# The first expert pair gathered in fp32 from x kept on chip, a norm weight as a column, and another order at the end of the first block's attention

## The chip, the cores and the metric

One Trainium2 chip, one of its cores. The metric is the device time of one execution in microseconds; the kernel is timed in several runs and their median is taken. A single execution has also been profiled.

## What is computed

256 tokens of width 1024 pass a first block (three mixers side by side, then a feed-forward net), a second block (two attentions with gates), a mixture of 32 experts in 4 groups, and a last norm. Cut to what the change touches:

```python
# first block: 6 GDN heads, 6 NSA heads, 4 pooling groups, concatenated, projected, added to x
o = rms_norm(o, norm_g) * jax.nn.silu(heads(z))          # gated norm of the GDN heads, norm_g is (64,)
y = jnp.concatenate([y_a, y_b, y_c], axis=-1)
x = x + y @ w_out
x = x + square(relu(rms_norm(x, norm_ffn) @ w_ffn1)) @ w_ffn2
# second block ends with x = x + (...) @ w_o; then, on h = rms_norm(x, g_moe):
#   a router picks 2 experts in each of the chosen groups, with weights;
#   x = x + sum over picked e of weight_e * ((silu(h @ w1[e]) * (h @ w3[e])) @ w2[e])
# out = rms_norm(x, g_final)
```

## The kernel before

The activations x lie on chip in the tile `xt` (128 partitions, two token tiles of 1024 fp32). Matmuls of the dense parts take operands split in two: `split` (L285 to L299) writes a high half `wh` (a copy with rounding, on POOL at L295 or on ACT at L297, in turn when no engine is named) and a low half `wl` (the difference, DVE, L298); three products, L302 to L304, make one full product. `lin_tok` runs such a product over eight chunks of rows.

The order of the first block is written by hand: `ORDER1` (L27) is a list of names, each of which advances one generator by a step. Names used below: `z` (the gate projection; SiLU parts on ACT, last step on DVE at L550), `fin` (finish of the GDN heads: the norm's scale `rO`, made on POOL at L312 from the sums `ssO` at L1273; the multiply y by rO at L1276; then per token tile z by the norm weights on POOL, L1284, and y by z on DVE, L1285; then six transposes `py` on PE at L1291, whose evacuations L1293 and L1294 make the two halves of `yT`), `pm` (pool mix: running sums on POOL at L683 to L689, a matmul at L693), `cmp` and `no` (the compressed branch of NSA and its output; `pcs` L910/L916, `poc` L941), `y` (load of w_out) and `o` (w_out itself, over chunks 6, 7, 0 to 5; chunks 6 and 7 need the pool mix alone).

The second block ends with `out` (L1582): w_o in column blocks; after each block `Router.part` (L1678) squares x (ACT, L1682), transposes it (`phT`, L1689), evacuates it to `hT` in turn on DVE and ACT (L1695, L1693), and makes the router's logits (`plg`, L1698); and `parts` (L1572 to L1580) splits x into three bf16 parts `xp` on POOL (copy, difference, copy, difference; L1577 to L1580). `finish` adds the residual x to the output banks on PE (L1717) and picks experts on DVE (L1729 to L1739, ending in the mask `A`), then ranks tokens with `prk` (PE, L1744).

`moe` (L1781) runs 16 pairs of experts with 64 slots each. Per pair: `slots` makes one-hot matrices `oh` (bf16 on DVE, L1815; an fp32 copy on ACT, L1820), `gather` picks the tokens by matmuls of xp with the one-hot matrix (six bf16 matmuls for each of eight chunks, L1829) and DVE writes `xe` (L1830); `first` makes `ph` with W1, `third` `ph3` with W3; `ppt` transposes the one-hot matrices, ACT copies them to `pT` (L1893) and applies SiLU (L1898), DVE multiplies into `a` (L1901), `pgt` transposes a (L1909), ACT evacuates it to `gT` (L1911), and `po_e` applies W2. The gather of the next pair lies ahead of and behind `pgt`. All expert matmuls are issued through the helper at L1802.

The experts' weights come in tiles of 1 MB (`Experts`, SLOTS of 23 tiles), issued on SP's queue in one fixed order; each transfer waits until what lay in its slot is no longer needed, and what stands behind it in the queue waits with it. 13 tiles are put ahead of the pairs, the rest of the first 23 as memory comes free at the end of the second block; from then on a slot is filled again when its pair has used it.

Of the kernel before, what the change touches and what calls it, by code (L numbers as in the profile page):

```python
# [108 lines left out]
def _params(I):  # L109
# [13 lines left out]
    rest = [("gng", row(I["gdn_norm"])),  # L123
# [22 lines left out]
_P2_SHAPES = (("gng", 64), ("qcol", 1), ("kcol", 3), ("krow", 64), ("posT", 32), ("w2c", 256), ("pw", 128), ("psc", 2))  # L146
# [23 lines left out]
def fused_kernel(ctx, tc, I, out, dbg=None):  # L170
# [36 lines left out]
    xt = cs2.tile([P, 2, D], F32, name="xt")  # L207
# [229 lines left out]
def block1(K):  # L437
# [4 lines left out]
    with ExitStack() as st1:  # L442
# [119 lines left out]
        def w_out():  # L562
# [402 lines left out]
class Gdn:  # L965
# [312 lines left out]
    def finish(self, z, yT):  # L1278
# [3 lines left out]
        for t in range(2):  # L1282
            zv = z[:, t].rearrange("p (h d) -> p h d", h=H)
            G.tensor_tensor(zv, zv, bc(K.PR("gng"), (P, H, 64), 1), op=OP.mult)  # L1284
            V.tensor_tensor(y[:, t], y[:, t], zv, op=OP.mult)  # L1285
            yield
        K.dump("y_a", y)
        for a in range(3):
# [4 lines left out]
            S.activation(yT[0][:, a], pf, AF.Copy)  # L1293
            V.tensor_tensor(yT[1][:, a], pf, yT[0][:, a].bitcast(F32), op=OP.subtract)  # L1294
# [14 lines left out]
def block2(K):  # L1309
# [4 lines left out]
    with ExitStack() as st:  # L1314
# [257 lines left out]
        def parts(i, t, c0, c1):  # L1572

            a, b, c = [K.xp[:, t, j, :, 16 * c0:16 * c1] for j in range(3)]
            x = xt[:, t, c0 * P:c1 * P].rearrange("p (q c) -> p c q", c=8)
            d = K.hp.tile([P, 512], F32, name="xd", bufs=2)[:, :(c1 - c0) * P].rearrange("p (c q) -> p c q", c=8)
            G.tensor_copy(a, x)  # L1577
            G.tensor_tensor(d, x, a, op=OP.subtract)
            G.tensor_copy(b, d)
            G.tensor_tensor(c, d, b, op=OP.subtract)  # L1580

        def out():  # L1582
            K.router = Router(K)
            for i, (c0, c1) in enumerate(OUT):
# [75 lines left out]
class Router:  # L1660
# [89 lines left out]
    def weights(self):  # L1750
# [14 lines left out]
        S.activation(gx, gx, AF.Exp)  # L1765
        x = x.rearrange("p t g e -> p t (g e)")
# [12 lines left out]
def moe(K):  # L1779
# [8 lines left out]
    with ExitStack() as st:  # L1788
# [3 lines left out]
        with tc.tile_pool(name="wx", bufs=1, reuse_waits="tile") as wx, \  # L1792
# [14 lines left out]

            def slots(p_):

                o = wx.tile([P, 2, 2, CAP], F32, name="oh")  # L1810
                ob = wx.tile([P, 2, 2, CAP], BF16, name="ohb")
                sl = bc(bc(C("IOTA1")[:, :CAP], (P, 2, CAP), 1), (P, 2, 2, CAP), 1)
                if p_ == 0:
                    for t in range(2):
                        V.scalar_tensor_tensor(ob[:, t], bc(rt.pr[:, t, :2], (P, 2, CAP), 2), 256.0, sl[:, t],  # L1815
                                               op0=OP.add, op1=OP.is_equal)
                    rt.last = V.scalar_tensor_tensor(rk, rt.pr, 256.0, rt.A.rearrange("p t g e -> p t (g e)"), op0=OP.add, op1=OP.mult)
                else:
                    V.tensor_tensor(ob, sl, bc(rk[:, :, 2 * p_:2 * p_ + 2], (P, 2, 2, CAP), 3), op=OP.is_equal)
# [322 lines left out]
```

## Time and profile before

| | |
|---|---|
| median of 3 runs | 1039.4 us (1038.61 to 1040.7) |
| profiled execution | 1036.04 us, span 1034.1 us |
| granted clock, mean | 0.99 |
| busy: PE, DVE, ACT, POOL | 989.6, 461.6, 277.3, 228.9 us |
| read from HBM | 289.87 MB |

Times in the rows below are microseconds from the start of the span. A row of a timeline has the start, the time to the end of the last instruction of the row, engine, line, operation, output and inputs, the count, and in brackets how long the engine had been idle and who released it. Wait rows give the engine and line that waited, whom it waited for, the total, the number of waits and the longest. [...]

### The profile page before, as it was taken

The page shows a single profiled execution, that of the slowest core. Times are in us where ns is not written, and L with a number is a line of the kernel's source. Part 1 is how long each engine was busy: PE and PEld are TensorE (multiplying, and loading weights), DVE is VectorE, ACT ScalarE, POOL GpSimd, SP SyncE. Part 2 cuts the span into 40 slices and gives each one's busy share as a digit, 9 for nine tenths or more (in the row PEclk, how much of TensorE's full clock was granted, in tenths as well). Part 3 has the DMA queues.
Part 4 walks back from the last instruction along what each step waited for, and adds up shares of the span by engine and source line. Part 5 has one row for each costly group of instructions (what it writes and reads, how often), then busy time and mean ns, then how long its engine had stood idle before and what let it go on. Part 6 is the DMA issues. An engine that isn't in the chain of part 4 may idle for free. (4 is left out here: it accounts for less than half of the span.)

```text
span 1034.1 us, 16556 instructions
## 1 busy us (share of the span) xinstructions
PE 989.6 (96%) x6613; PEld 686.2 (66%) x6613; DVE 461.6 (45%) x948; ACT 277.3 (27%) x635; POOL 228.9 (22%) x318
## 2 busy tenths in 40 slices
PE   7999988999999999999999899999999999999995
PEld 6778766899988888887788434444444555555352
DVE  3878866665566653567688511111111111111012
ACT  3543333433333342435343011111101111111012
POOL 3682442222222225443337400000000000000000
PEclk9999997999999999999999999999999999999998
DMA  9552363755555554365677799999999999999994
GB/s 345 146 167 94 107 182 129 282 176 191 184 189 198 177 170 153 123 204 175 222 259 312 272 394 421 420 419 420 421 421 418 421 420 421 419 419 420 420 410 179
DMA packets 81999, 292.61 MB, mean 283 GB/s; under 512 B 11584, under 2 KB 26240, under 8 KB 58880
## 3 DMA queue, kind: packets, MB, share of 16 engines
q1 hardware_dynamic: 80768, 289.68, 73.9%
q10 hardware_dynamic: 1152, 1.86, 0.5%
q8 instruction: 53, 0.87, 0.3%
q14 instruction: 26, 0.21, 0.1%
HBM read 289.87 MB, written 1.64 MB: 282 GB/s over the span
## 5 line engine op out<-in xcount | busy, mean ns | idle before, releaser
L1802 PE MATMUL ph<-w,xe 128*64 128x512 f32 x1024 | 227.0, 593 | 2.3 <-DMA w<-in_w_dram 2.3
L1802 PEld LDWEIGHTS ph<-w,xe 128*64 128x64 f32 x1024 | 85.5, 137 | 132.5 <-issue 124.7
L1802 PE MATMUL po_e<-w,gT 128*64 128x512 f32 x528 | 115.1, 584 | 0.7 <-ACT gT L1911 0.7
L298 DVE TENSOR_TENSOR wl<-ffn,wh 128x512 fp32r<-128x512 f32 (+1 forms) x100 | 84.6, 849 | 62.4 <-ACT wh L297 31.3
L312 POOL TENSOR_TENSOR r<-r4a,mhalf 128x2 f32<-128x2 f32 x1 | 0.7, 698 | 442.1 <-DVE r4a L310 442.1
L1896 DVE COPY ws<-ppt 64x2 f32<-64x2 f32 x32 | 5.0, 157 | 194.8 <-ACT pT L1893 194.6
L1802 PEld LDWEIGHTS po_e<-w,gT 128*64 128x64 f32 x528 | 40.1, 136 | 63.8 <-issue 55.9
L295 POOL TENSOR_SCALAR wh<-ffn 128x512 fp32r<-128x512 f32 (+1 forms) x50 | 44.5, 890 | 138.3 <-PE acc_c L405 61.1
L405 PE MATMUL acc_c<-xTfl,wh 128*128 128x256 f32 x256 | 70.2, 283 | 0.0
L404 PE MATMUL acc_c<-xTfh,wh 128*128 128x256 f32 x256 | 70.1, 283 | 0.0
L1893 ACT ACTIVATE pT<-ppt 128x256 fp32r<-128x256 f32 x16 | 6.1, 384 | 225.4 <-PE ppt L1802 225.4
L406 PE MATMUL acc_c<-xTfh,wl 128*128 128x256 f32 x256 | 64.6, 283 | 0.0
L297 ACT ACTIVATE wh<-ffn 128x512 fp32r<-128x512 f32 (+1 forms) x50 | 37.4, 751 | 84.9 <-PE acc_c L405 42.2
L303 PE MATMUL acc<-wl,hh 128*128 128x512 f32 x128 | 50.8, 397 | 0.0
L304 PE MATMUL acc<-wh,hl 128*128 128x512 f32 x128 | 50.6, 395 | 0.0
L405 PEld LDWEIGHTS acc_c<-xTfl,wh 128*128 128x128 f32 x256 | 49.0, 192 | 0.5
L404 PEld LDWEIGHTS acc_c<-xTfh,wh 128*128 128x128 f32 x256 | 48.8, 192 | 0.4
L1802 PE MATMUL pgat<-ohb,xp 128*128 128x128 bf16 x768 | 48.4, 219 | 0.5 <-DVE ohb L1815 0.5
L1802 PEld LDWEIGHTS <-xp 128*128 128x128 bf16 x768 | 44.5, 98 | 6.3 <-issue 6.1
L406 PEld LDWEIGHTS acc_c<-xTfh,wl 128*128 128x128 f32 x256 | 45.6, 192 | 0.1
L303 PE MATMUL acc_t<-wl,xT2h 128*128 128x512 f32 x96 | 39.6, 412 | 1.5 <-DVE wl L298 1.5
L1830 DVE TENSOR_TENSOR xe<-pgat,p 128x512 f32<-128x512 f32 (+1 forms) x34 | 22.4, 660 | 36.6 <-PE pgat L1802 36.6
(743 smaller groups left out, 1995.5 us busy)
## 6 DMA issues: line engine op xcount, KB each, us to landing
w<-in_w_dram SPq DMA_DIRECT2D x180, 1024.0 KB, 19.8
ffn<-in_w_ffn_dram SPq DMA_DIRECT2D x32, 1024.0 KB, 5.3
w<-in_w_dram SPq DMA_DIRECT2D x22, 512.0 KB, 10.2
w_gate<-in_w_in_dram SPq DMA_DIRECT2D x8, 1024.0 KB, 5.1
cmp_w<-in_cmp_w_dram SPq DMA_DIRECT2D x4, 1024.0 KB, 5.5
w_o<-in_w_o_dram SPq DMA_DIRECT2D x4, 1024.0 KB, 5.1
w_in_ks<-in_w_in_dram SPq DMA_DIRECT2D x2, 1024.0 KB, 10.3
w_out<-in_w_out_dram SPq DMA_DIRECT2D x4, 512.0 KB, 4.1
```

The costliest lines, as they stand in the source:

```text
L295: G.tensor_scalar(hi, w32, 1.0, 1.0, op0=OP.mult, op1=OP.mult)
L297: S.activation(hi, w32, AF.Copy)
L298: (G if eng == "p" else V).tensor_tensor(lo, w32, hi.bitcast(F32), op=OP.subtract)
L303: PE.matmul(o, a[0], b[1], start=False, stop=False)
L304: PE.matmul(o, a[1], b[0], start=False, stop=stop)
L404: PE.matmul(o, a[0], b[0], start=start, stop=False, skip_group_check=True)
L405: PE.matmul(o, a[0], b[1], start=False, stop=False, skip_group_check=True)
L406: PE.matmul(o, a[1], b[0], start=False, stop=stop, skip_group_check=True)
L1802: last[0] = PE.matmul(*a, **k).ins
L1830: V.tensor_tensor(xe[:, c0:c0 + n], pg, bc(gmo[:, c0:c0 + n], (P, n, P), 2), op=OP.mult)
L1893: S.activation(pT, ppt[:, :2 * P].rearrange("p (t s) -> p t s", t=2), AF.Copy)
L1896: V.tensor_copy(ws[64 * g:64 * g + 64], ppt[64 * g:64 * g + 64, 2 * P + g:2 * P + 3:2 - g])
```

## The change

1. In `ORDER1` both steps of the pool mix (`pm`) follow directly behind `y`; their later places are taken out.
2. The norm weights of the GDN heads are loaded as one column instead of a row of 64; the multiply of z on POOL (L1284) goes, and the weights become the scale of the evacuations of `py` (an activation with scale, and a scalar_tensor_tensor in place of a tensor_tensor).
3. w_out's high halves are all made on ACT (`eng="a"`), where before POOL and ACT took turns.
4. `xt` lies in a pool that lasts to the end; from the second pair on its memory holds `a`, `gT` and `xe`. The shared tiles `o4` go from 5 to 4.
5. `parts` goes. In its place `exact` makes the same three parts in eight pieces of 256 columns: copies on ACT, differences on POOL, the differences behind the router's weights.
6. The first pair gathers in fp32 straight from `xt`, two fp32 matmuls a chunk, with an fp32 one-hot matrix that DVE writes itself. SiLU's table is loaded behind the router's exponentials (`pre`), and `third` of the first pair comes after `ppt` and the SiLU activation.

```diff
-          "sco sol a1 sco sco a1 u kc rec z a2 cmp u u rec a1 a0 u u a2 a3 rec rec u a3 cmp rec a5 a2 y pm cmp "
-          "rec z z a5 prep z a3 z z cmp pm fin rec a5 no fin o pm fin no")
+          "sco sol a1 sco sco a1 u kc rec z a2 cmp u u rec a1 a0 u u a2 a3 rec rec u a3 cmp rec a5 a2 y pm pm cmp "
+          "rec z z a5 prep z a3 z z cmp fin rec a5 no fin o fin no")
...
-    rest = [("gng", row(I["gdn_norm"])),
+    rest = [("gng", np.tile(np.asarray(I["gdn_norm"]).reshape(-1), 2)),
...
-    xt = cs2.tile([P, 2, D], F32, name="xt")
+    xt = cst.tile([P, 2, D], F32, name="xt")
...
-                yield from K.lin_tok(yT, wo[k], 512, sp, ev, order=(6, 7, 0, 1, 2, 3, 4, 5))
+                yield from K.lin_tok(yT, wo[k], 512, sp, ev, order=(6, 7, 0, 1, 2, 3, 4, 5), eng="a")
...
-            zv = z[:, t].rearrange("p (h d) -> p h d", h=H)
-            G.tensor_tensor(zv, zv, bc(K.PR("gng"), (P, H, 64), 1), op=OP.mult)
-            V.tensor_tensor(y[:, t], y[:, t], zv, op=OP.mult)
+            V.tensor_tensor(y[:, t], y[:, t], z[:, t].rearrange("p (h d) -> p h d", h=H), op=OP.mult)
...
-            S.activation(yT[0][:, a], pf, AF.Copy)
-            V.tensor_tensor(yT[1][:, a], pf, yT[0][:, a].bitcast(F32), op=OP.subtract)
+            S.activation(yT[0][:, a], pf, AF.Copy, scale=K.PR("gng"))
+            V.scalar_tensor_tensor(yT[1][:, a], pf, K.PR("gng"), yT[0][:, a].bitcast(F32), op0=OP.mult, op1=OP.subtract)
...
-                if i < len(OUT) - 1:
-                    for t in range(2):
-                        parts(i, t, c0, c1)
-            i = K.router.logits()
-            with tc.issue_after(i.ins):
-                for t in range(2):
-                    parts(len(OUT) - 1, t, *OUT[-1])
+            K.router.logits()
...
         S.activation(gx, gx, AF.Exp)
+        S.activation(small((1,), "pre"), gx[:, 0, :1], AF.Silu)
...
+            xv = K.xt.rearrange("p t (h n) -> p (t h) n", h=2)
+
+            def o4(dt=F32, name="o4"):
+                return wx.tile([P, 512], dt, name=name, tag="o4", bufs=4)
+            xd = []
+
+            def exact(c, t):
+
+                pa, pb, pc = [xp[:, t, j, :, 32 * c:32 * c + 32] for j in range(3)]
+                x = K.xt[:, t, 256 * c:256 * c + 256].rearrange("p (q c) -> p c q", c=8)
+                if not xd:
+                    xd.append(o4(name="xd"))
+                d = xd[0][:, 256 * t:256 * t + 256].rearrange("p (c q) -> p c q", c=8)
+                S.activation(pa, x, AF.Copy)
+                G.tensor_tensor(d, x, pa, op=OP.subtract)
+                S.activation(pb, d, AF.Copy)
+                G.tensor_tensor(pc, d, pb, op=OP.subtract)
...
+                        if len(oh) == 1:
+                            mm(pg[:, k], K.xt[:, t, c0 + k::8], oh[0][:, t], start=t == 0, stop=t == 1)
+                            continue
...
             with tc.issue_after(rt.last.ins):
                 rt.weights()
+                for c in range(4):
+                    for t in range(2):
+                        exact(c, t)
...
-                if not end:
+                if 0 < p_ < NPAIR - 1:
                     third()
...
-                a = wx.tile([P, 512], F32, name="a", tag="o4", bufs=5)
+                a = xv[:, 0]
                 S.activation(a, ph, AF.Silu, scale=ws[:, 1:2])
-                if end:
+                if p_ in (0, NPAIR - 1):
                     third()
```

The schedule sets where the pieces come to stand. DVE at the end of the first block's attention, around the GDN norm (osq and ssO are the squares and their sums, rO the scale, z the gate, wl low halves of w_out), before and then with the change:

```order
L1270 TENSOR_TENSOR osq_1880<-y_a 128x384
L895 COPY vcr<-pvc 96x128
L298 TENSOR_TENSOR wl<-w_out_2116,wh 128x512
L550 SCALAR_TENSOR_TENSOR z<-zth,z 128x192 x2
L1272 TENSOR_REDUCE ssO<-osq_1880 128x6
L1285 TENSOR_TENSOR y_a<-y_a,z 128x384
L1273 SCALAR_TENSOR_TENSOR ssO<-ssO,aq 128x6
L1276 TENSOR_TENSOR y_a<-y_a,rO 128x384
L298 TENSOR_TENSOR wl<-w_out_2116,wh 128x512
L1285 TENSOR_TENSOR y_a<-y_a,z 128x384
```

```order
L1273 SCALAR_TENSOR_TENSOR ssO<-ssO,aq 128x6
L298 TENSOR_TENSOR wl<-w_out_2114,wh 128x512
L695 SCALAR_TENSOR_TENSOR yTl<-pyc,p_82,yTh 128x256 x2
L1276 TENSOR_TENSOR y_a<-y_a,rO 128x384
L298 TENSOR_TENSOR wl<-w_out_2114,wh 128x512
L550 SCALAR_TENSOR_TENSOR z<-zth,z 128x192 x3
L1283 TENSOR_TENSOR y_a<-y_a,z 128x384
L550 SCALAR_TENSOR_TENSOR z<-zth,z 128x192
L310 TENSOR_SCALAR krra<-kss 32x1
L870 SCALAR_TENSOR_TENSOR ht<-htt,hth 128x64
L1283 TENSOR_TENSOR y_a<-y_a,z 128x384
```

The norm's sums (ssO) and the multiply by rO now stand ahead of the last steps of the gate z; behind the last step of z there is one multiply of y by z.

On PE in the same place, twelve matmuls of w_out (chunks 6 and 7) stand ahead of py where six stood, and the pool mix's matmuls pyc, which stood behind py, come before the last step of z.

POOL at the router (r: the scale of the router's norm, xp and xd: the three parts of x and the differences, W, gx and den: the router's weights), before and then with the change:

```order
L312 TENSOR_TENSOR r_6146<-r3a,mhalf 128x2
L1577 CAST xp<-xt 128x8x32 x2
L1578 TENSOR_TENSOR xd<-xt,xp 128x256 x2
L1579 CAST xp<-xd 128x8x32 x2
L1580 TENSOR_TENSOR xp<-xd,xp 128x8x32 x2
L1762 TENSOR_TENSOR W<-lg,m_6627 128x64
L1763 TENSOR_TENSOR gx<-lg,gm 128x8
```

```order
L312 TENSOR_TENSOR r_6144<-r3a,mhalf 128x2
L1745 TENSOR_TENSOR W<-lg,m_6586 128x64
L1746 TENSOR_TENSOR gx<-lg,gm 128x8
L1751 TENSOR_TENSOR W<-W,A 128x64
L1807 TENSOR_TENSOR xd<-xt,xp 128x256 x2
L1756 TENSOR_TENSOR W<-W,den 128x64
L1809 TENSOR_TENSOR xp<-xd,xp 128x8x32 x2
```

The parts stood between the norm's scale and the router's weights, and also, not shown, between the splits of w_o ahead of it; now none stands ahead of the weights, and the differences of the eight pieces follow.

PE in the first pair (pgat: gather, ph and ph_6707 or ph_6677: the products with W1 and W3, ppt: transposes of the one-hot matrices), before:

```order
L1802 MATMUL ph_6707<-w_2_6541,xe 64x512
L1802 MATMUL ph_6707<-w_2_6543,xe 64x512
L1886 MATMUL ppt<-c_69,oh 128x128 x2
L1802 MATMUL ppt<-Wr,oh 128x3 x2
L1802 LDWEIGHTS xp
L1802 MATMUL pgat<-ohb,xp 128x128
```

and with the change:

```order
L1786 MATMUL ph<-w_2_4586,xe 64x512
L1786 MATMUL ph<-w_2_6503,xe 64x512
L1899 MATMUL ppt<-c_69,oh 128x128 x2
L1786 MATMUL ppt<-Wr,oh 128x3 x2
L1786 MATMUL ph_6677<-w_2_6505,xe 64x512
L1786 MATMUL ph_6677<-w_2_6507,xe 64x512
```

The products with W3 now stand behind ppt; the gather of the next pair follows them.

## Rows read from the trace of the kernel before

**Rows 1.** The page: busy time of the engines, granted clock and DMA in 40 slices.

```profile
PE 989.6 (96%) x6613; PEld 686.2 (66%) x6613; DVE 461.6 (45%) x948; ACT 277.3 (27%) x635; POOL 228.9 (22%) x318
...
PEclk9999997999999999999999999999999999999998
DMA  9552363755555554365677799999999999999994
```

**Rows 2.** Windows (us, busy time and count of each engine, granted clock, DMA).

```profile
core 0: us, PE busy (x) PEld busy (x) DVE busy (x) ACT busy (x) POOL busy (x), PEclk, DMA share, GB/s
...
700.00:800.00 100.00, 100.00 (x624) 46.75 (x622) 16.07 (x34) 11.48 (x22) 0.00 (x0) 1.00 1.01 420
```

**Rows 3.** Waits of PE from 600 us on (total, times, longest).

```profile
PE ph L1802 <- DMA w<-in_w_dram: 2.3, 2, 1.3
```

**Rows 4.** Timeline of PE, end of the first attention (start, busy, idle before).

```profile
152.69 0.44 PE L1291 MATMUL py<-c,y_a 128*128 128x128 f32 x2 [0.66 <-DVE y_a L1285]
157.18 0.69 PE L1291 MATMUL py<-c,y_a 128*128 128x128 f32 x2 [4.05 <-DVE y_a L1285]
158.58 0.69 PE L1291 MATMUL py<-c,y_a 128*128 128x128 f32 x2 [0.72 <-DVE yTl L1294]
...
172.94 0.68 PE L941 MATMUL poc<-pcTs,vcr 32*64 32x256 f32 x12 [0.68 <-ACT pcTs L935]
174.85 0.47 PE L302 MATMUL acc_t<-wh,yTh 128*128 128x512 f32 x1 [1.23 <-ACT yTh L943]
```

**Rows 5.** Window in the same stretch, columns as in the windows above.

```profile
155.65:169.30 13.65, 11.40 (x48) 8.43 (x49) 6.95 (x22) 2.68 (x7) 3.71 (x6) 0.50 0.21 77
```

**Rows 6.** Timeline of POOL in the same stretch.

```profile
148.39 1.24 POOL L1284 TENSOR_TENSOR z<-z,p 128x384 f32<-128x384 f32 x1 [2.39 <-DVE z L550]
...
153.21 1.33 POOL L312 TENSOR_TENSOR rO<-ssO,mhalf 128x6 f32<-128x6 f32 x1
```

**Rows 7.** Timeline of DVE in the same stretch.

```profile
154.57 0.97 DVE L1276 TENSOR_TENSOR y_a<-y_a,rO 128x384 f32<-128x384 f32 x1 [1.45 <-POOL rO L312]
...
156.58 0.55 DVE L1285 TENSOR_TENSOR y_a<-y_a,z 128x384 f32<-128x384 f32 x1
```

**Rows 8.** Window of w_o in the second block.

```profile
553.80:572.60 18.80, 17.22 (x135) 15.87 (x133) 15.44 (x23) 6.48 (x18) 18.22 (x23) 1.00 0.73 284
```

**Rows 9.** Groups by line, DVE between 100 and 135 us (busy, mean ns).

```profile
L298 DVE TENSOR_TENSOR wl<-w_in_u,wh 128x256 fp32r<-128x256 f32 x7 | 2.9, 422 | 2.9 <-POOL wh L295 2.9
```

**Rows 10.** Groups by line, 553.8 to 581 us, DVE and POOL (busy, mean ns).

```profile
L298 DVE TENSOR_TENSOR wl<-w_o,wh 128x256 fp32r<-128x256 f32 x14 | 12.0, 893 | 1.7 <-POOL wh L295 1.7
...
L1578 POOL TENSOR_TENSOR xd<-xt,xp 128x256 f32<-128x256 f32 x4 | 3.6, 904 | 0.0
...
L1580 POOL TENSOR_TENSOR xp<-xd,xp 128x256 bf16<-128x256 f32 x4 | 2.6, 668 | 0.0
```

**Rows 11.** Timeline of PE, router and first pair.

```profile
573.81 1.08 PE L1698 MATMUL plg<-p,hT 128*128 128x36 f32 x8 [0.47 <-DVE hT L1695]
...
580.51 0.20 PE L1744 MATMUL prk<-A,cu 128*128 128x64 bf16 x1 [3.38 <-DVE A L1739]
...
582.57 1.50 PE L1802 MATMUL pgat<-ohb,xp 128*128 128x128 bf16 x24 [0.46 <-DVE ohb L1815]
...
589.37 10.52 PE L1802 MATMUL ph<-w,xe 128*64 128x512 f32 x48
...
604.17 0.75 PE L1909 MATMUL pgt<-c,a 128*128 128x128 f32 x4 [2.20 <-DVE a L1901]
```

**Rows 12.** Timeline of ACT, first pair.

```profile
601.35 1.28 ACT L1898 ACT_TABLE_LOAD   x1
```

**Rows 13.** Waits of the DMA queue, 570 to 612 us (total, times, longest).

```profile
SPq L1652 <- PE ph L1802: 15.6, 4, 7.6
...
SPq L1652 <- POOL xp L1580: 4.8, 1, 4.8
```

**Rows 14.** The page's groups by line: a half of a split on ACT.

```profile
L297 ACT ACTIVATE wh<-ffn 128x512 fp32r<-128x512 f32 (+1 forms) x50 | 37.4, 751 | 84.9 <-PE acc_c L405 42.2
```

More of the change, by code (lines that the diff above doesn't have):

```diff
@@ L145 @@
 _P1_SHAPES = (("g_mix", 8), ("cwT", 36), ("alog", 6), ("dtb", 6), ("wba", 240))
-_P2_SHAPES = (("gng", 64), ("qcol", 1), ("kcol", 3), ("krow", 64), ("posT", 32), ("w2c", 256), ("pw", 128), ("psc", 2))
+_P2_SHAPES = (("gng", 1), ("qcol", 1), ("kcol", 3), ("krow", 64), ("posT", 32), ("w2c", 256), ("pw", 128), ("psc", 2))
 _P3_SHAPES = (("g_moe", 8),)
@@ L1570, in mix @@
                 K.hp = st.enter_context(tc.tile_pool(name="hp", bufs=1, reuse_waits="tile"))
[L1572 to L1580, printed above, removed]
         def out():
@@ L1806, in then @@
                 return tc.issue_after(last[0])
+            xv = K.xt.rearrange("p t (h n) -> p (t h) n", h=2)
[12 more added lines that the diff above has]
+                G.tensor_tensor(pc, d, pb, op=OP.subtract)
             def slots(p_):
                 o = wx.tile([P, 2, 2, CAP], F32, name="oh")
+                if p_ == 0:
+                    for t in range(2):
+                        V.scalar_tensor_tensor(o[:, t], bc(rt.pr[:, t, :2], (P, 2, CAP), 2), 256.0,
+                                               bc(C("IOTA1")[:, :CAP], (P, 2, CAP), 1), op0=OP.add, op1=OP.is_equal)
+                    rt.last = V.scalar_tensor_tensor(rk, rt.pr, 256.0, rt.A.rearrange("p t g e -> p t (g e)"), op0=OP.add, op1=OP.mult)
+                    return [o.rearrange("p t g s -> p t (g s)")]
                 ob = wx.tile([P, 2, 2, CAP], BF16, name="ohb")
                 sl = bc(bc(C("IOTA1")[:, :CAP], (P, 2, CAP), 1), (P, 2, 2, CAP), 1)
[L1813 to L1819, printed above, removed]
+                V.tensor_tensor(ob, sl, bc(rk[:, :, 2 * p_:2 * p_ + 2], (P, 2, 2, CAP), 3), op=OP.is_equal)
                 S.activation(o, ob, AF.Copy)
@@ L1827, in gather, with xtile @@
                     for t in range(2):
+                        if len(oh) == 1:
+                            mm(pg[:, k], K.xt[:, t, c0 + k::8], oh[0][:, t], start=t == 0, stop=t == 1)
+                            continue
                         for j in range(3):
                             mm(pg[:, k], xp[:, t, j, c0 + k], oh[1][:, t], start=t == 0 and j == 0, stop=t == 1 and j == 2)
-                V.tensor_tensor(xe[:, c0:c0 + n], pg, bc(gmo[:, c0:c0 + n], (P, n, P), 2), op=OP.mult)
-            def xtile():
-                return wk.tile([P, 8, P], F32, name="xe")
+                xo = xe[c0 // 4][:, c0 % 4:c0 % 4 + n] if type(xe) is list else xe[:, c0:c0 + n]
+                V.tensor_tensor(xo, pg, bc(gmo[:, c0:c0 + n], (P, n, P), 2), op=OP.mult)
+            def xtile(p_):
+                if p_ == 0:
+                    return [o4(name="xe").rearrange("p (c s) -> p c s", c=4) for _ in range(2)]
+                return xv[:, 2:4].rearrange("p h (c s) -> p (h c) s", c=4)
             def first(o, xe, Wx, c0=0, n=8):
@@ L1837, in first @@
                     for g in range(2):
-                        mm(o[64 * g:64 * g + 64], xe[:, c, 64 * g:64 * g + 64], Wx[g][c // 4][:, c % 4],
+                        xc = xe[c // 4][:, c % 4] if type(xe) is list else xe[:, c]
+                        mm(o[64 * g:64 * g + 64], xc[:, 64 * g:64 * g + 64], Wx[g][c // 4][:, c % 4],
                                   start=c == 0, stop=c == 7)
-            oh, xe = slots(0), xtile()
+            oh, xe = slots(0), xtile(0)
             gather(oh, xe, 0, 2)
@@ L1844, in moe @@
                 rt.weights()
+                for c in range(4):
+                    for t in range(2):
+                        exact(c, t)
             def scatter(todo, stop):
@@ L1902, in moe @@
                 if not end:
-                    oh, xe = slots(p_ + 1), xtile()
+                    oh, xe = slots(p_ + 1), xtile(p_ + 1)
                     with then():
@@ L1909, in moe @@
                         last[0] = PE.transpose(pgt[:, c], a[:, c::4], idn).ins
-                gT = wx.tile([P, 4, P], F32, name="gT", tag="o4", bufs=5)
+                gT = xv[:, 1].rearrange("p (c s) -> p c s", c=4)
                 S.activation(gT, pgt, AF.Copy)
@@ L1930, in moe @@
                 for i, (n, q) in enumerate(cols):
-                    oh_ = wx.tile([P, 512], F32R, name="oh_", tag="o4", bufs=5)[:, q]
-                    ol_ = wx.tile([P, 512], F32R, name="ol_", tag="o4", bufs=5)[:, q]
+                    oh_, ol_ = [o4(F32R, k)[:, q] for k in ("oh_", "ol_")]
                     S.activation(oh_, po[i][:, q], AF.Copy)
@@ L1950, in squares @@
                 for t in range(2):
-                    junk = wk.tile([P, 512], BF16, name="junk4", tag="xe")
+                    junk = wk.tile([P, 512], BF16, name="junk4")
                     S.activation(junk, y[t][n], AF.Square, accum_out=ss[:, t, n:n + 1])
```

## The prediction

> **What bounds the kernel now.** I read the page first, then windows, then the waits of PE and of the DMA queue, then timelines where PE stands still. PE is busy 96% of the span, and the granted clock is full in all slices but one, early, which shows 7 tenths [rows 1]. DMA is half idle in the first block and at full share from the 24th of the 40 slices on, that is from about 595 us [rows 1]. A window of 100 us there shows both at once: PE busy 100%, DMA share 1.01, 420 GB/s [rows 2]. So behind 600 us two chains run side by side, the expert products on PE and the stream of weights, and neither has slack worth much: from 600 us on PE waits for weights 2.3 us in all [rows 3]. Nothing in the change touches the pace of the pairs behind the first. What it can win, it wins ahead of 606 us, and it is kept only if the stream of weights comes earlier by as much. The stream's slots are freed by PE in program order, so a shift of PE in the first block shifts the stream as well.
>
> PE stands still in three places that the change touches.
>
> The end of the first attention: PE waits 0.66 and 4.05 us for y_a, 0.72 for yTl, 0.68 for pcTs and 1.23 for yTh [rows 4], together 7.3 us. Behind the 4.05 us the clock is 0.50, that is 1.2 GHz, for 13.65 us, in which PE is busy 11.40 [rows 5]; at full clock half of that, 5.7 us, would not be there. Place and price together: 13.0 us. The wait for y_a is a chain through two engines: POOL makes rO at 153.21, 1.33 us [rows 6], DVE, which stood 1.45 us for it, multiplies by rO (0.97) and, behind a low half of w_out, by z (0.55, at 156.58) [rows 7].
>
> w_o in the second block: 18.80 us with PE busy 17.22, POOL busy 18.22 [rows 8], so PE is idle 1.6 us. POOL is full with the parts of x, and DVE beside it takes 893 ns for a low half that took 422 elsewhere [rows 9, 10].
>
> The router and the first pair: 3.38 us until the mask A, 0.46 until the one-hot matrix, 2.20 until a [rows 11]; SiLU's table load, 1.28 us, lies in the last of these [rows 12].
>
> **The change part by part.** The profiled execution took 1036.0 us, 3.4 below the median of the runs; the sum is a shift and I apply it to the median.
>
> *End of the first attention.* The POOL multiplies (1.24 us for the one shown, a second like it) go [rows 6], and, by the order on DVE, the norm's sums and rO lie ahead of the last steps of z, so that behind z only one multiply, 0.55 us [rows 7], leads to py; PE has six more matmuls of w_out to do meanwhile, which cost nothing since they are only taken forward. The folded weight costs nothing: the evacuations of py are the same in number and size. Of the waits I leave 0.72, 0.68 and 1.23, which hang on later chains (2.6 us), and 2.4 us for y_a, since DVE still makes three steps of z and two low halves there and ACT, not POOL, now makes w_out's high halves. That is 5.0 us of waits and no loss of clock: **-8.0 us**. Lower bound: waits of 5 us and the clock as low as before for the same stretch, -2.3. Upper: only 3.5 us of waits remain, -9.5. I take the value nearer to the upper end because the 4.05 us that stood right ahead of the fall of the clock are the ones removed; the 3.38 us ahead of the router's ranking [rows 11] were followed by a full clock.
>
> *High halves on ACT.* Eight of sixteen move from POOL to ACT, 0.75 us each on the mean [rows 14], 6 us of ACT work over some 30 us of PE; ACT is busy 2.68 of 13.65 us there [rows 5]. Cost nothing, covered by that idle time; without the cover it is the slow rival below.
>
> *w_o.* POOL loses 15 us of parts, ACT takes eight copies of 256 columns. PE can win at most its idle 1.6 us; I take -1.0, and +0.5 for the copies that stand ahead of the last hT on ACT. Bounds -1.6 and +1.
>
> *Router.* DVE's chain to A runs beside POOL's parts. If its steps between two tiles shrink as the low half does (893 to 422 [rows 9, 10]), the wait of 3.38 us halves: -1.7, bounds 0 and -3.4. The multiply into xe now stands behind the router's small DVE steps: +1.0, about twice the 0.46 us that PE stood for the one-hot matrix behind the same steps [rows 11], bounds 0 and 1.5.
>
> *Gather.* 48 bf16 matmuls, 24 in 1.50 us [rows 11], 3.0 us, become 16 fp32 ones, and an fp32 matmul shows as two instructions. The nearest row is the router's product, eight instructions with a new stationary tile each in 1.08 us, 0.135 each: 32 make 4.3 us, **+1.3**. Upper bound by pgt, fp32 with strided columns like the new gather: four in 0.75, 0.19 each, +3.0; lower bound 0. In that row each instruction brings a new stationary tile and still takes 0.135 us with its load, so the loads lie beside the matmuls or are as short as they. [...]
>
> *First pair.* The table load goes behind the router's exponentials and the 32 instructions with W3, the second part of 48 in 10.52 us [rows 11] or 7.0 us, now cover SiLU: the 2.20 us go, **-2.0**, bounds 0 and -2.2. This holds if ACT has finished the parts by then. They are eight pieces; POOL takes 0.90 + 0.67 us a piece [rows 10], 12.6 us from some 580 us on, ACT's second copies between. That ends by about 594, ahead of the end of W3's products. If POOL's chain takes 1.5 times as long, ACT's pT and SiLU stand in line behind it and PE waits 5 us: the third rival.
>
> *DMA.* SP's order is the same. A wait of 4.8 us for the parts [rows 13] goes, so three tiles are asked for earlier, ahead of the longest wait for the first pair, 7.6 us [rows 13]. The slice ahead of 595 us has DMA at seven tenths [rows 1], which lets the stream follow PE's shift; no extra term. A norm row less is loaded at the start: nothing, covered by the first block's half-idle DMA [rows 1].
>
> Sum: -8.0 - 1.0 + 0.5 - 1.7 + 1.0 + 1.3 - 2.0 = **-9.9 us**. 1036.0 - 9.9 = 1026.1 in a profiled execution like this one; 1039.4 - 9.9 = **1029.5 us** for the median.
>
> **The rivals.** *The clock still falls (or another wait takes over).* y_a comes in time, but the chain of the compressed branch or yTh keeps PE waiting and the clock goes to 0.50 for a stretch two thirds as long: 13.0 - 5.0 - 3.8 = 4.2 us won there, with the rest -1.9: 1033.3 us. For it: 1.23 and 0.68 us of those waits stand untouched. Against: each is far shorter than 4.05.
>
> *ACT becomes the bound* (slower). All high halves of w_out stand in ACT's queue behind PT, z and the exponentials, which wait for PE, while PE waits for the halves. If each of the eight moved ones makes PE wait its own 0.75 us [rows 14], 6.0 us come to the 13.0 that stay, since y_a is no earlier on PE when PE itself is late, and with the other terms, -1.9, the kernel takes 1043.5 us. It turns the sign from 0.24 us a moved half on if the first term is lost, from 1.2 us if it is kept. Against it stands ACT's idle time in the window [rows 5].
>
> *The first pair pays.* The parts come late (5 us, above) or the gather runs at the upper bound and more: 1034 to 1037 us. [...]
>
> **How the numbers follow.** Forecast 0.68, clock or another wait 0.16, first pair 0.09, ACT 0.07. Differences under 0.2%, 2 us, can't be told from no change here. The forecast's own bounds: its best ends (-9.5, -1.6, -3.0) give 1024, its weaker ones 1033. The range takes in the second and most of the third case: 1023.5 to 1036.5. Faster by over 0.2%, below 1037.4: nearly all of the forecast (0.66), most of the second case (0.14), six tenths of the third (0.06), 0.86; the rest of these lies within 0.2% (0.06) but for 0.01, and with the slow rival 0.08 is left for slower.
>
> **What would show it.** Right: no slice under full clock near 155 us; PE's wait for y_a under 2.5 us; no parts on POOL ahead of the router's weights and a wait of PE for A near 1.7; a gather of 32 fp32 instructions in 4 to 5 us; no wait for a in the first pair; the start of the second pair earlier by as much as the end. Wrong: a granted clock of 0.50 at the same place; waits of PE for wh from ACT; PE waits for weights behind 600 us that grow by what was won before.

## The result, and the profile after

The changed kernel takes 1022.3 us in the median of four runs (1019.5 to 1023.4), against 1039.4 before; the ratio is 0.983 with a 95% interval of 0.9808 to 0.9852. It is faster by 17.1 us where 9.9 were forecast, and it lies just under the range. One execution among all the runs below, of the change with the first block turned back, took 1421.2 us at a mean granted clock of 0.653 and is left out. The profiled execution after has 1019.54 us and a span of 1017.7, against 1036.04 and 1034.1.

The page of the kernel after, which answers to [rows 1], and its window of 100 us, which answers to [rows 2]:

```profile
PE 986.4 (97%) x6597; PEld 688.4 (68%) x6597; DVE 451.4 (44%) x948; ACT 288.4 (28%) x659; POOL 210.3 (21%) x300
...
PEclk9999999999999999999999999999999999999998
DMA  9552377565555455446667799999999999999994
GB/s 344 146 163 89 107 205 282 186 200 191 182 190 184 166 176 166 146 146 219 218 255 296 294 411 424 426 424 425 427 423 426 423 427 423 427 425 425 425 415 175
```

```profile
700.00:800.00 100.00, 100.00 (x615) 46.65 (x613) 16.39 (x33) 11.30 (x21) 0.00 (x0) 1.00 1.01 425
```

No slice is under full clock until the last. PE is busy 100% behind 600 us as before, but the stream of weights moves 425 GB/s where it moved 420. Neither a shorter wait nor an earlier start explains a rate of transfer over 200 us and more; the forecast had no term for it.

Where PE stands at the same instructions, from the timelines of PE in the two kernels (us from the start of the span):

| instruction on PE | before | after | shift |
|---|---|---|---|
| w_out goes on behind poc | 174.85 | 163.46 | -11.4 |
| first phT (second block's w_o) | 554.78 | 543.29 | -11.5 |
| last phT | 572.57 | 559.73 | -12.8 |
| prk | 580.51 | 566.09 | -14.4 |
| first ph, first pair | 584.09 | 571.32 | -12.8 |
| pgt, first pair | 604.17 | 591.94 | -12.2 |
| pgt, last pair | 1012.02 | 996.01 | -16.0 |

So 11.4 us come from the end of the first attention. From there to the router's ranking (prk) 3.0 more are won, of which the first pair loses 2.2 again. Between the first pair's pgt and the last pair's 3.8 us more come, and 0.4 behind that. For the 3.8 the forecast had no term.

The timeline of PE at the end of the first attention, after (start, busy, idle before), which answers to [rows 4]:

```profile
148.93 1.09 PE L813 MATMUL po<-PT,ksw 128*64 128x128 f32 x14 [1.12 <-ACT PT L805]
...
152.84 0.60 PE L1289 MATMUL py<-c,y_a 128*128 128x128 f32 x4
...
156.47 0.38 PE L1289 MATMUL py<-c,y_a 128*128 128x128 f32 x2
...
161.84 0.68 PE L941 MATMUL poc<-pcTs,vcr 32*64 32x256 f32 x12 [0.70 <-ACT pcTs L935]
...
163.46 0.50 PE L302 MATMUL acc_t<-wh,yTh 128*128 128x512 f32 x1 [0.94 <-ACT yTh L943]
```

All waits are 1.12, 0.70 and 0.94 us; py starts without one, and the granted clock is 1.00 from 148 to 176 us. The same stretch on POOL and DVE, which answers to [rows 6, 7]:

```profile
145.25 1.33 POOL L312 TENSOR_TENSOR rO<-ssO,mhalf 128x6 f32<-128x6 f32 x1 [6.14 <-DVE ssO L1273]
```

```profile
146.99 0.55 DVE L1276 TENSOR_TENSOR y_a<-y_a,rO 128x384 f32<-128x384 f32 x1
...
148.97 0.55 DVE L1283 TENSOR_TENSOR y_a<-y_a,z 128x384 f32<-128x384 f32 x1
...
149.90 0.54 DVE L1283 TENSOR_TENSOR y_a<-y_a,z 128x384 f32<-128x384 f32 x1
```

rO is made at 145.25, 8 us earlier than before, and lies 3.7 us ahead of the multiply by z. The two multiplies by the gate are ready at 149.5 and 150.4, and PE comes to py at 152.84, held by nothing but the matmuls of w_out.

The timeline of PE at the router and the first pair, after, which answers to [rows 11]:

```profile
566.09 0.20 PE L1727 MATMUL prk<-A,cu 128*128 128x64 bf16 x1 [1.03 <-DVE A L1722]
...
567.53 3.86 PE L1786 MATMUL pgat<-oh,xt 128*128 128x128 f32 x16
571.32 1.94 PE L1786 MATMUL ph<-w,xe 128*64 128x512 f32 x8
573.19 2.17 PE L1786 MATMUL pgat<-oh,xt 128*128 128x128 f32 x8
...
577.16 2.18 PE L1786 MATMUL pgat<-oh,xt 128*128 128x128 f32 x8
...
583.57 7.09 PE L1786 MATMUL ph<-w,xe 128*64 128x512 f32 x32
590.59 1.51 PE L1786 MATMUL pgat<-ohb,xp 128*128 128x128 bf16 x24
591.94 0.70 PE L1922 MATMUL pgt<-c,xt 128*128 128x128 f32 x4
```

The wait for A is 1.03 us in place of 3.38, and the wait of pgt for a is gone. But the gather takes 3.86 + 2.17 + 2.18 = 8.2 us in place of 3.2 (24 bf16 instructions in 1.50 and twice 12 in 0.84).

### The profile page after: what moved, and what is told of

It is laid out like the page before. It is cut to its first block, busy times and chain, and to the rows that moved or that the text cites. A ratio compares the mean times of both kernels' runs of the same rounds, so it can differ in the third digit from the quotient of the medians.

```text
span 1017.7 us, 16524 instructions
## 1 busy us (share of the span) xinstructions
PE 986.4 (97%) x6597; PEld 688.4 (68%) x6597; DVE 451.4 (44%) x948; ACT 288.4 (28%) x659; POOL 210.3 (21%) x300
## 3 DMA queue, kind: packets, MB, share of 16 engines
HBM read 289.84 MB, written 1.64 MB: 286 GB/s over the span
## 5 line engine op out<-in xcount | busy, mean ns | idle before, releaser
L1786 PE MATMUL ph<-w,xt 128*64 128x512 f32 x960 | 211.4, 593 | 0.0
L1786 PEld LDWEIGHTS ph<-w,xt 128*64 128x64 f32 x960 | 81.3, 137 | 121.0 <-issue 118.9
L1786 PE MATMUL po_e<-w,xt 128*64 128x512 f32 x528 | 115.1, 584 | 0.7 <-ACT xt L1924 0.7
L1786 PEld LDWEIGHTS po_e<-w,xt 128*64 128x64 f32 x528 | 40.1, 136 | 63.8 <-issue 56.2
L1786 PE MATMUL pgat<-ohb,xp 128*128 128x128 bf16 x720 | 45.3, 219 | 0.0
L1786 PEld LDWEIGHTS <-xp 128*128 128x128 bf16 x720 | 41.7, 98 | 4.7 <-issue 4.5
L304 PE MATMUL acc_t<-wh,xT2l 128*128 128x512 f32 x96 | 38.0, 396 | 0.0
## 6 DMA issues: line engine op xcount, KB each, us to landing
w<-in_w_dram SPq DMA_DIRECT2D x22, 512.0 KB, 10.2
```

The costliest lines, as they stand in the source:

```text
L304: PE.matmul(o, a[1], b[0], start=False, stop=stop)
L1786: last[0] = PE.matmul(*a, **k).ins
```

## The experiments

In each, the kernel before ran beside the kernel under test on the same chip; a ratio is to those runs. There are three such groups: the four kernels with parts of the change; the two with one unused tile of 4 bytes, the one with all slots at multiples of 64 and the first one of the gather; and the last four. In them the kernel before had medians of 1037.9, 1037.1 and 1040.0 us, so kernels are compared within a group where it can be done. Over all runs it took 1035.5 to 1041.4 us.

**The parts: first block and experts.** First the kernel before with the order, the norm weight as a column and w_out's high halves on ACT:

```diff
-          "sco sol a1 sco sco a1 u kc rec z a2 cmp u u rec a1 a0 u u a2 a3 rec rec u a3 cmp rec a5 a2 y pm cmp "
-          "rec z z a5 prep z a3 z z cmp pm fin rec a5 no fin o pm fin no")
+          "sco sol a1 sco sco a1 u kc rec z a2 cmp u u rec a1 a0 u u a2 a3 rec rec u a3 cmp rec a5 a2 y pm pm cmp "
+          "rec z z a5 prep z a3 z z cmp fin rec a5 no fin o fin no")
...
-            zv = z[:, t].rearrange("p (h d) -> p h d", h=H)
-            G.tensor_tensor(zv, zv, bc(K.PR("gng"), (P, H, 64), 1), op=OP.mult)
-            V.tensor_tensor(y[:, t], y[:, t], zv, op=OP.mult)
+            V.tensor_tensor(y[:, t], y[:, t], z[:, t].rearrange("p (h d) -> p h d", h=H), op=OP.mult)
...
-                yield from K.lin_tok(yT, wo[k], 512, sp, ev, order=(6, 7, 0, 1, 2, 3, 4, 5))
+                yield from K.lin_tok(yT, wo[k], 512, sp, ev, order=(6, 7, 0, 1, 2, 3, 4, 5), eng="a")
```

> The kernel before with all three edits to the first block (pool mix first, norm weight as a column, w_out's high halves on ACT) and nothing of the second block or the experts. Theory (the first block's end carries the gain): the start of the feed-forward on PE 11.4 us earlier than before, no stretch under full clock near 155 us, the end 11 to 15 us earlier (1024 to 1028 for a before of 1039). Rival (the expert part carries a third or more, through an earlier stream of weights): the end at most 10 us earlier although the feed-forward is 11.4 earlier, with PE waiting for weights near the end.

Measured: 1026.6 us, ratio 0.9887 (0.9861 to 0.9912), which is 11.7 us of the 1037.9 that the kernel before took beside it. The feed-forward starts 10.8 us earlier, the clock is full near 155 us, and PE still waits 1.9 us for weights near the end: the rate is 420 GB/s. In this profile the clock also fell at 112 us (0.57 for 4 us), which it did not in the profiles of before and after, and PE comes to the stretch 0.5 us later than with the whole change (po, L813, at 146.51 against 146.00); from there on it is as fast.

Then the change with the same lines turned back, of which one is:

```diff
-                yield from K.lin_tok(yT, wo[k], 512, sp, ev, order=(6, 7, 0, 1, 2, 3, 4, 5), eng="a")
+                yield from K.lin_tok(yT, wo[k], 512, sp, ev, order=(6, 7, 0, 1, 2, 3, 4, 5))
```

> The change with the three edits to the first block undone. Theory: the first half as before with the clock at 0.50 near 155 us; the second pair starts 0.9 us earlier than before (the difference measured between feed-forward and first pair), and the end 1 to 2 us earlier, about 1038. Rival (earlier stream of weights from the expert part): the end 4 to 5 us earlier, about 1035, without waits for weights behind 950 us.

Measured: 1033.2 us in six runs, ratio 0.9939 (0.9919 to 0.9959), 6.3 us by the ratio and 4.6 by the medians. In the profile the first pair's pgt comes 0.5 us later than before and the end only 2.0 us earlier, since its clock fell at places where that of before did not (its mean is 0.986, that of before 0.990; its feed-forward starts 1.1 us later, and behind the last pgt it loses 1.3). Between these two places, from the start of the feed-forward to the last pgt, it is 4.4 us shorter: 0.5 up to the first pair's pgt, 3.8 behind it, with a rate of 425 GB/s and no wait for weights. The rival's number holds, but the stream is faster and not only earlier. The two parts together (0.9887 times 0.9939 is 0.9827) give the whole.

**Inside the first block.** The kernel before with the order alone (the four lines of `ORDER1` above and nothing else), of which the second pair is:

```diff
-          "rec z z a5 prep z a3 z z cmp pm fin rec a5 no fin o pm fin no")
+          "rec z z a5 prep z a3 z z cmp fin rec a5 no fin o fin no")
```

> The kernel before with the pool mix first in the order and no other edit. Theory (the order alone moves the norm's scale ahead of the gate and gives PE six more matmuls to do, the multiplies on POOL cost little): PE waits under 2.5 us for y_a, full clock, the feed-forward 9 to 11 us earlier, end 8 to 11 us earlier. Rival (the multiplies on POOL and the splits there hold y_a): the wait stays above 3.5 us, the clock still falls, the end at most 4 us earlier.

and with the other two edits, without the order:

```diff
-            G.tensor_tensor(zv, zv, bc(K.PR("gng"), (P, H, 64), 1), op=OP.mult)
...
+                yield from K.lin_tok(yT, wo[k], 512, sp, ev, order=(6, 7, 0, 1, 2, 3, 4, 5), eng="a")
```

> The kernel before with the norm weight as a column and w_out's high halves on ACT, the old order of the pool mix. Theory: the norm's scale still stands behind the gate, so PE waits about 3 us for y_a and the clock falls or not by chance of that; end 1 to 5 us earlier. Rival (POOL's load was what held y_a): wait under 1.5 us, full clock, end 8 us or more earlier.

Measured: the order alone 1029.7 us, 0.9925 (0.9896 to 0.9953), feed-forward 10.2 us earlier; column and ACT without it 1036.1 us, 0.9982 (0.9967 to 0.9997), feed-forward 2.1 us earlier. The timeline of PE with the order alone, and DVE's second multiply by z:

```profile
153.04 0.60 PE L1291 MATMUL py<-c,y_a 128*128 128x128 f32 x4
...
156.43 0.38 PE L1291 MATMUL py<-c,y_a 128*128 128x128 f32 x2
...
164.60 0.47 PE L302 MATMUL acc_t<-wh,yTh 128*128 128x512 f32 x1 [1.09 <-ACT yTh L943]
```

```profile
152.30 0.56 DVE L1285 TENSOR_TENSOR y_a<-y_a,z 128x384 f32<-128x384 f32 x1 [0.91 <-POOL z L1284]
```

and with the column and ACT alone, and a window of it in which the clock fell:

```profile
152.69 0.38 PE L1289 MATMUL py<-c,y_a 128*128 128x128 f32 x2
156.15 0.44 PE L1289 MATMUL py<-c,y_a 128*128 128x128 f32 x2 [3.08 <-DVE y_a L1283]
...
160.18 0.69 PE L1289 MATMUL py<-c,y_a 128*128 128x128 f32 x2
```

```profile
148.00:176.00 28.00, 22.39 (x134) 17.39 (x133) 19.40 (x48) 11.33 (x26) 7.94 (x11) 0.82 0.37 132
```

With the old order PE has six matmuls, comes to py 3.1 us too soon, and the clock falls in the stretch that follows (0.82 over 28 us). With the new order the multiplies of z on POOL are still there and PE doesn't wait for them, if only just: DVE waits 0.91 us for the second one and ends its multiply at 152.86, PE comes to py at 153.04. The order is what carries the term. What the other two edits add is read from the same matmul on PE ahead of the stretch (po, L813) to the feed-forward, which leaves out the fall of the clock at 112 us: 29.9 us with the order alone, 28.7 with all three edits and in the change, so 1.2 us. The end with the order alone is 7.0 us earlier in the profile, not 10.2: in this execution the clock also fell at the router and behind pgt (0.71 from 570 to 575 us, 0.66 from 595 to 600), where it did not in that of before, and PE waits 2.8 us for weights instead of 2.3.

**The stream of weights.** What differs in the expert part for a transfer is where it goes. The programs' tables of tile addresses show it (the traces hold no addresses): the small tile `pre`, 4 bytes, lies above the slots on the right side of memory, takes 32 bytes there, and pushes 13 of the 23 slots down by as much.

```
start of the 13 right slots     before 32 past a multiple of 256     after 0 past
start of the 10 left slots      six 192 past, four 160 past          the same
```

An unused tile of the same size was put into either kernel, in the router's `weights`; nothing reads or writes it.

```diff
+        small((1,), "pad")
```

> The kernel before with one unused tile of 4 bytes beside the router's small tiles; it moves 13 of the 23 weight slots by 32 bytes, from 32 past a multiple of 64 bytes to a multiple of 64; no instruction is added or moved. Theory (the stream of weights is faster into slots that start on a multiple of 64 bytes, and the change's new tile `pre` does this by accident): 425 GB/s in place of 420 behind 600 us, waits for weights near the end gone, end 3 to 5 us earlier. Rival (the faster stream comes from the expert part's less memory traffic): 420 GB/s and the time of before within 1 us.

> The change with such an unused tile, which moves the 13 slots to 32 past a multiple of 64. Theory: 421 GB/s or less (17 of 23 slots off, as in the kernel before), PE waits 2 to 4 us for weights near the end, time 1026 against 1022. Rival: 425 GB/s and 1022.

Measured: the kernel before with the pad 1035.2 us, 0.9972 (0.9958 to 0.9985); the change with the pad, which puts the 13 slots 224 bytes past a multiple of 256, 1026.6, 0.9885 (0.9864 to 0.9907). The change itself did not run in this group; its version with all slots on multiples of 64 (below), at its rate, took 1022.7, 0.9856. A window of 200 us of the first, and of the second with its wait for weights:

```profile
700.00:900.00 200.00, 200.00 (x1204) 97.52 (x1202) 30.15 (x62) 22.18 (x42) 0.00 (x0) 1.00 1.01 425
```

```profile
700.00:900.00 200.00, 200.00 (x1238) 100.26 (x1238) 32.83 (x67) 24.46 (x47) 0.00 (x0) 1.00 1.01 420
```

```profile
PE ph L1787 <- DMA w<-in_w_dram: 3.0, 3, 1.3
```

The rate follows the address, in both directions and with the instructions as they were: 425 with the slots at a multiple of 256, 420 without. The time follows: 2.9 us by the ratio and 1.9 by the medians for the kernel before, where 3 to 5 were expected; 3.0 by the ratios and 3.9 by the medians between the two versions of the change. The profiles agree. From the first pair's pgt to the last pair's PE takes, over all fourteen of them:

| rate behind 600 us | kernels | first pgt to last pgt, us | mean |
|---|---|---|---|
| 420 or 421 GB/s | 6 | 407.7 to 409.7 | 408.7 |
| 425 | 6 | 404.0 to 405.6 | 404.7 |
| 426 | 2 | 403.4, 404.2 | 403.8 |

So the stream is worth about 4 us, whichever expert part or first block stands with it. (Two of the first six and one of the second have a fall of the clock right behind the first pgt in their times.)

Which multiple counts was asked with three more kernels: all slots at multiples of 64 (the first line below alone), all at multiples of 256 (the first and the second), and the 13 slots at 128 past one (the third).

```diff
+            wx.tile([P, 1], F32, name="pad")
...
+    cst.tile([P, 16], F32, name="pad64")
...
+        small((32,), "pad")
```

> The change with an unused tile ahead of the last four slots, which brings all 23 to multiples of 64 bytes. Theory: 426 to 427 GB/s; since PE never waits for weights behind the first pair in the change, the end moves by less than 1 us. Rival (as above): 425, no change.

> The change with two unused tiles that bring the start of all 23 weight slots to multiples of 256 bytes (in the change 13 of 23 are; in the run that made all of them multiples of 64 only, the rate stayed at 425). Theory (what counts is a start on a multiple of 256 bytes): the rate behind 600 us rises by 10/13 of the step from 420 to 425, to about 429 GB/s; PE sets the end, so the time stays within 1 us of the change. Rival (a multiple of 64, and the ten slots on the left side don't matter): 425.

> The change with an unused tile that moves the 13 slots from multiples of 256 to 128 past one. Theory (256 bytes): 420 GB/s, waits of 2 to 4 us for weights near the end, time 1026. Rival (64 or 128 bytes are enough): 425 GB/s, time of the change.

Measured: 1022.7 us and 425 GB/s, where 426 to 427 were expected; 1022.0 and 426; 1025.5 and 421. Windows of 200 us, of the multiples of 256 and of 128 past:

```profile
700.00:900.00 200.00, 200.00 (x1237) 100.00 (x1237) 32.98 (x67) 24.38 (x47) 0.00 (x0) 1.00 1.01 426
```

```profile
700.00:900.00 200.00, 200.00 (x1238) 100.34 (x1239) 32.70 (x66) 24.45 (x47) 0.00 (x0) 1.00 1.01 421
```

The third takes 3.5 us more than the second, run beside it, and has PE waiting 2.6 us for weights again. 128 past (421 GB/s) is nearly as bad as 32 or 224 past (420 both), so multiples of 64 or 128 are not enough, and a start on a multiple of 256 is what the 13 slots gain from. The size was wrong for the other ten: with all on multiples of 256 the step is 1.4 GB/s (426.3 against 424.9 as the mean of sixteen windows), not 4. So for these 13 slots the runs show that the start counts and what it costs; why it costs that, and why ten slots at 160 and 192 past cost so little, they don't show.

**The gather.** The same number of instructions, with neighbouring columns as the stationary tile; it leaves out that the rows of W1 and W3 would have to come in the same order.

```diff
-                            mm(pg[:, k], K.xt[:, t, c0 + k::8], oh[0][:, t], start=t == 0, stop=t == 1)
+                            mm(pg[:, k], K.xt[:, t, (c0 + k) * P:(c0 + k + 1) * P], oh[0][:, t], start=t == 0, stop=t == 1)
```

> The change with the first pair's gather taking 128 neighbouring columns of x as its stationary tile in place of every eighth column; the first pair is fed wrong columns, all counts and sizes are the same. Theory (the load of a stationary tile whose columns lie 32 bytes apart takes 334 ns against 191 for neighbouring ones and sets the pace): the gather's 32 instructions take 3.6 to 4.5 us in place of 8.2, the second pair starts about 4 us earlier, end 3 to 4 us earlier. Rival (fp32 with a new stationary tile each time is slow in itself): the gather stays near 8 us.

Measured: 1020.5 us, 0.9831 (0.9809 to 0.9853); its profile has the first pair's pgt, and so the second pair, 4.0 us earlier than the change's. The end gains less than the 3 to 4 us expected: 2.1 by the median against 1022.7 of the kernel at the same rate run beside it, 1.9 between the two profiles. There the last pgt is 3.5 us earlier, and 1.7 are lost behind it, where the clock is 0.82 and 0.75 in the 8 us from 992 on. The groups by line of PE's weight loads between 560 and 600 us (busy, mean ns), of the change and then of this kernel, and the gather in its timeline:

```profile
L1786 PEld LDWEIGHTS pgat<-oh,xt 128*128 128x128 f32 x32 | 7.9, 334 | 1.6 <-issue 1.6
...
L1700 PEld LDWEIGHTS y<-xt,c 128*128 128x128 f32 x16 | 2.9, 191 | 0.3
```

```profile
L1786 PEld LDWEIGHTS pgat<-oh,xt 128*128 128x128 f32 x32 | 3.9, 191 | 1.7 <-issue 1.6
```

```profile
567.36 1.95 PE L1786 MATMUL pgat<-oh,xt 128*128 128x128 f32 x16
...
571.18 1.16 PE L1786 MATMUL pgat<-oh,xt 128*128 128x128 f32 x8
...
574.14 1.16 PE L1786 MATMUL pgat<-oh,xt 128*128 128x128 f32 x8
```

A load of columns 32 bytes apart takes 334 ns, of neighbouring ones from the same tile 191, and the gather goes from 8.2 to 4.3 us. That is the stride and nothing else: as many instructions load as many full tiles. The length of one load is not what it adds to the time: the 32 loads of 191 ns have a busy time of 3.9 us, less than their sum of 6.1, so they overlap one another. With a step of 16 bytes pgt's loads take 209 ns in the same window of the change; why a step of 32 takes so much longer than one of 16, no run shows.

**A version that beats both.** Neighbouring columns are right if the rows of the first pair's W1 and W3 come in the same order, and the norm weights (`g_moe0`) as well.

```diff
-            src = w.rearrange("(p c) n -> p c n", c=c)
+            src = w.rearrange("(c p) n -> p c n" if p == 0 and nm != "w2_2" else "(p c) n -> p c n", c=c)
...
+                gm_ = gmo if len(oh) > 1 else PR("g_moe0")
```

> The change with the first pair's gather from 128 neighbouring columns, and the rows of that pair's W1 and W3 loaded in the same order, so that all that is computed is as in the change. Theory (the gather costs 4 us less and nothing else changes): as in the run with the wrong columns, gather 4.3 us, second pair 4 us earlier, end 2 to 4 us earlier, 1018 to 1020. Rival (the transfers of W1 and W3 in pieces of 2 KB are slow): the eight tiles of the first pair land later, PE waits for them or for the stream at the end, no gain.

> Both: the gather from neighbouring columns and all slots on multiples of 256 bytes. Theory: 429 GB/s and the end as in the run with the gather alone or up to 1 us earlier, 1017 to 1020, since PE sets it. Rival (weights set the end once PE is 4 us earlier): 2 us or more below the run with the gather alone.

Measured: 1017.9 us, 0.9793 (0.9772 to 0.9813), and with all slots on multiples of 256 1018.7, 0.9788 (0.9766 to 0.981). The change with nothing but the addresses moved took 1022.0 beside them (0.9806 to 0.9848), so both are 3 to 4 us below it, with intervals that overlap by a third of their width or less. The rows of 2 KB cost nothing that shows: the rate behind 600 us is 425 GB/s in the first, as in the change. The two can't be told apart: with PE 4 us earlier one wait of 1.1 us for weights came back in the first, none in the second, and the second's profile lost more than that to the clock (0.991 on the mean against 0.997), which is under full at 112 and 548 us and right behind the last pgt, where the first's is not. The 429 GB/s expected of the second were 426.

## Why the prediction was too small

*End of the first attention: right in mechanism, -8.0 forecast, -11.4 measured, outside the bound of -9.5.* The step that failed is the 2.4 us left for y_a, "since DVE still makes three steps of z and two low halves there and ACT, not POOL, now makes w_out's high halves". py waits for nothing. Of the 5.0 us of waits forecast to remain, 1.64 are measured (0.70 for pcTs and 0.94 for yTh), which makes 13.0 - 1.64 = 11.4: the 0.72 for yTl went too, as other matmuls of PE, w_out's among them, stand between py's second and third part. A wait that the forecast didn't name, for PT ahead of w_out, grew from 0.47 us, in the timeline of PE before,

```profile
149.34 1.09 PE L813 MATMUL po<-PT,ksw 128*64 128x128 f32 x14 [0.47 <-ACT PT L805]
```

to 1.12. The clock stayed full there, as said. The traces give the granted clock as a share of full speed, 0.50 for 13.65 us in the profile of before [rows 5]; the forecast's 5.7 us are half of the busy time at that share. They need no frequency in GHz, and no run shows one. Of the causes named, the order is the one that counts: alone it gives 10.2. The POOL multiplies and the high halves on ACT, between which no run tells, give the other 1.2.

*High halves on ACT: nothing, as said.* The rival in which ACT becomes the bound fell: no wait for wh in that stretch.

*w_o: -1.0 + 0.5 forecast, -0.6 measured* (-1.35 up to the last phT, +0.8 for hT).

*Router: -1.7 forecast, -2.35 measured* at prk: DVE's largest step took 0.69 us beside an idle POOL, where it took 1.34. *xe: +1.0 forecast, -0.6 measured*: no wait for xe came, and the 0.46 us for the one-hot matrix went.

*Gather: +1.3 forecast with an upper bound of 3.0, +5.0 measured.* The row taken, the router's product, has neighbouring columns; the one taken for the bound, pgt, has columns 16 bytes apart, and the gather's lie 32 apart. The bound was called one for "strided columns like the new gather" and had half the stride. This term, too, lies outside its bounds; in the sum it hid part of what the rest won.

*First pair: -2.0 forecast; the 2.20 are gone.* The parts were done at 579.6, ahead of ppt. Whether the table load or W3's products did it was not tried.

*DMA: "no extra term".* This is the other step that failed, with "Nothing in the change touches the pace of the pairs behind the first". The stream's rate was taken as given, but it hangs on where the slots lie, and a tile of 4 bytes moved them: 3.8 us between the two profiles, 3.5 to 3.9 between medians of kernels run side by side. The change had been read for its instructions, not for its addresses. The waits for weights, 2.3 us, had been read, but no term took them as something that could go.

*The base.* The profiled execution before was a light one. Four other profiles have the old first pair: the kernel before with the pad, with the first block's three edits, with the order alone, and with column and ACT. In them PE waits 3.46 or 3.47 us for A, and in all four the clock fell behind this wait; in three it fell behind the 2.20 us of pgt as well (0.54 from 606.9 to 610.6 us in the first of them, 0.66 and 0.69 over 5 us with the order alone and with column and ACT). Of the first of them, the timeline of PE, and a window:

```profile
580.96 0.24 PE L1744 MATMUL prk<-A,cu 128*128 128x64 bf16 x1 [3.47 <-DVE A L1739]
...
581.06 2.91 PE L1717 MATMUL y<-xt,c 128*128 128x256 f32 x6
584.43 2.53 PE L1803 MATMUL pgat<-ohb,xp 128*128 128x128 bf16 x24 [0.46 <-DVE ohb L1816]
...
606.98 1.13 PE L1910 MATMUL pgt<-c,a 128*128 128x128 f32 x4 [2.20 <-DVE a L1902]
607.90 2.76 PE L1803 MATMUL pgat<-ohb,xp 128*128 128x128 bf16 x24
```

```profile
581.00:587.00 6.00, 5.54 (x34) 4.51 (x36) 1.69 (x12) 0.79 (x3) 0.77 (x3) 0.53 0.96 355
```

There the residual's six instructions take 2.91 us, not 1.54, and the gather 2.53, not 1.50. In the profile of before the clock stayed full behind 3.38 us [rows 11] (1.00 from 581 to 584.1 us), and the prediction reckoned with that alone. From prk to the first pair's pgt PE takes 23.7 us in the profile of before, 24.9 to 26.0 in the four others, and 25.8 or 25.9 in the six profiles that have the change's first pair and strided gather, none of which shows a fall there. So in these four the waits that the change removes are worth 1.2 to 2.4 us more than in the one execution that the forecast was built on. The mean clocks of the other runs fit this, though they don't say where a fall lies: of 42 runs of the kernel before, 13 show 0.983 or 0.984 and took 1039.9 to 1041.4 us, 21 show 0.989 to 0.991, like the profile, and took 1035.5 to 1037.7; no run of the change or of a version of it with both its parts is under 0.991.

In sum, between the two profiles 16.4 us were won where 9.9 were forecast. The two mis-sized terms (3.4 us won beyond the forecast at the first block, 3.7 lost beyond it at the gather) cancel, which was luck. The small ones (w_o, router, xe, first pair) add 2.6, and the missing one, the stream, adds 3.8, with 0.4 behind the last pgt. The other 0.7 to the 17.1 between the medians are not more than such runs differ by. Two of the signs named in advance failed with these terms: the gather takes 8.2 us, not 4 to 5, and the second pair is 12.2 us earlier, not as much as the end. And one reading of the page was incomplete: the last slice of the kernel before is under full clock as well, as it is after the change [rows 1].

## What to carry to other kernels

Read where the destinations of a long stream of transfers start before and after a change: a tile of a few bytes allocated above them can move them off, or onto, a multiple of 256 bytes, and here, for 13 slots of 23, that was 1.2% of the rate (420 against 425 GB/s) and about 4 us. Price a strided stationary tile by a row with that very stride: here a load took 191 ns with neighbouring columns, 209 with a step of 16 bytes, 334 with one of 32. Where two engines feed a chain, look first at what the order lets them do early; here moving the pool mix gave 10.2 of the first block's 11.4 us, the instructions removed and those moved to ACT the rest. And look at more than one profile of the kernel before: one in five had the clock full behind the wait that the change removes.

## What was not expected of the hardware

The stream of 1 MB transfers ran at 420 to 421 GB/s with 13 of its 23 slots 32, 128 or 224 bytes past a multiple of 256, and at 425 with these 13 on one, in all twelve such profiles; bringing the ten slots at 160 and 192 past onto multiples as well added 1.4 GB/s in the other two. A 128x128 fp32 stationary tile loads in 191 ns with neighbouring columns, 334 with columns 32 bytes apart. And a wait of PE of 3.4 to 3.5 us was followed by a full clock in one execution and, in four others, by a mean granted clock of 0.53 to 0.76 over the 6 us from prk on.
